# The end of two expert mixtures: residual rows reloaded before the last two scatters, whose rows TensorE places on their tokens with 0/1 matrices

## The chip, the cores and the metric

One core of one Trainium2 chip runs the whole program. The time is that of one execution in device microseconds; the kernel before has a median of 1824.23 us in 3 runs (1823.89 to 1829.28).

## The reference

Two layers of a transformer (a mixer and a mixture of experts each) are followed by a third block. There are 512 tokens of width 1024, all in float32. The mixture and what follows it:

```python
x = x + g_f * hierarchical_moe(hf, ...)          # 16 experts, two per token
# inside: hid = silu(t @ w_gate) * (t @ w_up);  y = (hid * gate) @ w_down
hm = rmsnorm(x, norm_mix[1]) * (1 + sc_m) + sh_m  # next layer: x feeds a norm at once
y = forgetting_mixer(hm, b_w_in, ...)             # projection by b_w_in
...
h = rmsnorm(x, norm_g)                            # after the second mixture: second_block
proj = h @ w_in + b_in
```

So each mixture ends in a sum over tokens (x plus the experts' rows), and what follows normalises that sum and multiplies it by a weight matrix. There are two such places in the program. The **first end** lies between the first mixture and `mix_b` (the second layer's mixer, about 905 to 960 us), the **second end** between the second mixture and `block2` (about 1455 to 1500 us).

## The kernel before, in words

Tokens stand in four tiles of 128 rows (x0 to x3, here also tile 0 to tile 3). `moe` runs 17 steps; step e computes the hidden layer of expert e and then, in `expert_out`, the output rows of expert e-1. An expert has at most 96 tokens (`CAP`); their numbers are the column `tidx` of that expert. The output rows `y` (96 x 1024) go out on POOL's queue by an indirect DMA that adds them in memory to the residual array `xd`:

```python
self.scatter(R["xd"], idx, y)      # last line of expert_out
```

The 16 scatters follow one another, since all of them add to `xd`. "Scatter 13" below is that of expert 13, and 14 and 15 are the last two.

After the mixture `normed_T` loads the four tiles from `xd` into new buffers `xl` (SP's queue), multiplies each by the norm's row (DVE, `hn`), takes the squares' sum on ACT (`tn_j`, in `tile_norm`), scales `hn` on DVE, and hands it to `transpose_tile`: eight transposes on PE (`tp`), then for each half the upper part of the split on ACT (`hThi`) and the lower part on DVE (`hTlo`). The next phase multiplies these by weights that are split alike: a staged tile `wst` (loaded on SP's queue) becomes `whi` on ACT (L316) and `wlo` on DVE (L317). In `mix_b` a unit is four such tiles of 128x768 and there are four `wst` buffers (`weight_pool(4, 8)`); in `block2` a tile is 128x1024 and there are three (`weight_pool(3, 5)`). w0 and w1 are the first two units. In `mix_b` w0 meets tile 0 alone and then both meet tile 1 and tile 2; in `block2` the first products need tiles 0 and 1 together (256 columns).

SP's queue issues the loads in program order, and each engine its own instructions in the order that the scheduler has fixed beforehand (PE's by hand). Memory of closed pools is used again: the first writer of a new tile waits for whatever still uses the old one.

Of the kernel before, what the change touches and what calls it, by code (L numbers as in the profile page):

```python
# [20 lines left out]
S = 512  # L21
# [91 lines left out]
class Kernel:  # L113
# [948 lines left out]
                res.append([hi, lo])  # L1062
        return res

    def expert_out(self, pool, hT, d, idx, gate, R):

        nc, q = self.nc, self.CAP
        y = self.t(pool, [q, D], F32, "y", 4)
        for n in range(2):
            p = self.sc()[:q]  # L1070
            ns = slice(n * 512, (n + 1) * 512)
            for j in range(2):
                h, w = hT[j], d[j][0]
# [148 lines left out]
    def moe(self, R, after):  # L1222
# [3 lines left out]
        with ExitStack() as ctx:  # L1226
# [27 lines left out]
                self.token_gates(ohs, [R["tg"][:, t, e, 2:5] for t in range(NT)], gates[:, e:e + 1], self.CAP)  # L1254

            xs = {}

            def step(e, ohs):
                if e < 16:
                    w = self.W[e]  # L1260
                    p = self.mm()
                    self.expert_part(p, xs[e], w, range(4))
                    if e < 15:
                        xs[e + 1] = self.expert_in(pm, xgs[(e + 1) % 3])
                    self.expert_part(p, xs.pop(e), w, range(4, KC))
                    listed(e + 3, True)
                    hid = self.expert_hidden(pm, p)
                if e:
                    w = self.W[e - 1]
                    self.expert_out(pm, self.hT, w[4:], idx[:, e - 1:e], gates[:, e - 1:e], R)  # L1270
                if e < 16:
                    self.hT = self.expert_hidden_T(pm, hid, self.W[e])
                    load(6)
# [14 lines left out]
            with self.tc.manual_schedule(engines={mybir.EngineType.PE}):  # L1288
                for e in range(17):
# [3 lines left out]
                    if e == 15:  # L1293
                        self.ln_table = None
                        self.need_ln(self.last_act)
        self.rt_ctx.close()
        return R["xd"]

    def normed_T(self, pool, xd, rows, hT):

        nc = self.nc
        xs = []
        for t in range(NT):
            xs.append(self.t(pool, [P, D], F32, "xl", NT))
            self.x_ins = nc.sync.dma_start(xs[t], xd[t * P:(t + 1) * P, :])
        yield
        for t, x in enumerate(xs):
            h = self.t(pool, [P, D], F32, "hn", 2)
            nc.vector.tensor_mul(h, x, rows[0])
            r = self.tile_norm(pool, x)  # L1310
            if rows[1] is None:
                nc.vector.tensor_scalar(h, h, r, None, op0=ALU.mult)
            else:
                nc.vector.scalar_tensor_tensor(h, h, r, rows[1], op0=ALU.mult, op1=ALU.add)
            self.transpose_tile(h, hT, t)
            yield

    def close_rows(self):
        self.rp_ctx.close()
        self.rp = None  # L1320

# [107 lines left out]
        yield from self.attn_values(pool, "b", blocks, hs, terms, lambda h, o: nc.scalar.activation(oT[hs[h], hp], o, AF.Copy))  # L1429
        u["done"] = 2  # L1430

    def mix_b(self, xd, rows):
        nc = self.nc
        w = self.a["b_w_in"]
        NC = 3 * D + 16
        unit = lambda hp: self.w_unit(w, hp * P, NC, D)
# [5 lines left out]
        with ExitStack() as ctx:  # L1442
# [13 lines left out]
            with self.tc.manual_schedule(engines={mybir.EngineType.PE}):  # L1456
                with ExitStack() as c2:
                    pn = self.pool(c2, "pn")
                    w0 = unit(0)
                    split(w0)  # L1460
                    tiles = self.normed_T(pn, xd, rows, hT)
# [377 lines left out]
                yield 1.25 * m  # L1839
        return p[:, :m]  # L1840

    def block2(self, xd, grow):
        nc, a = self.nc, self.a
        ud = self.t(self.dp, [4 * P, 4, P], F32, "ud")
        yd = self.t(self.dp, [4 * P, 4, P], F32, "yqd")
        bcol = lambda blk: self.vcol("bin")[:, blk:blk + 1]
        with ExitStack() as ctx:
# [16 lines left out]
            with self.tc.manual_schedule(engines={mybir.EngineType.PE}):  # L1864
# [4 lines left out]
                with ExitStack() as c2:  # L1869
# [1 line left out]
                    todo = []  # L1871
                    w0 = self.proj_w(0, todo)
                    split(todo)
                    tiles = self.normed_T(pn, xd, (grow, None), hT)
# [225 lines left out]
    def right_pools(self):  # L2100
# [5 lines left out]
        self.ws = self.pool(self.rt_ctx, "ws", "right")  # L2106

    def load_x(self, pool, src):
        xs = []
# [99 lines left out]
    def start(self, ctx):  # L2209
        self.pools(ctx)  # L2210
        self.rp_ctx = ctx.enter_context(ExitStack())
        self.rt_ctx = ctx.enter_context(ExitStack())
        self.rp, self.ln_table = None, None
        self.have_params = False
        self.wp_ctx = ctx.enter_context(ExitStack())
# [37 lines left out]
```

## Time and profile before

| | us |
|---|---|
| median of 3 runs | 1824.23 |
| lowest and highest | 1823.89, 1829.28 |
| the profiled execution | 1824.57 |
| its span | 1822.6 |
| PE busy | 1624.6 (89%) |
| DVE, ACT, POOL busy | 1285.6, 919.7, 123.9 |

The profiled execution is 0.34 us above the median, so its rows can stand for all of them. PE has most of the busy time, but the share is a mean: at both ends of a mixture PE stands still while the residual goes out, comes back and is normalised. Times in the trace count from the span's start.

### The profile page before, as it was taken

What the parts mean: (1) busy time and instruction counts of PE and PEld (TensorE: products, weight loads), DVE (VectorE), ACT (ScalarE), POOL (GpSimd) and SP (SyncE); (2) the same over time, 40 slices, a digit from 0 to 9 for tenths busy, and PEclk for the clock granted to TensorE, in tenths of its full rate; (3) what the DMA queues carried; (4) which work ended last, traced back from release to release, by engine and by line L of the source; (5) the groups of instructions that cost most, each with busy time, mean ns of one, the idle gap of its engine ahead of it and who ended that gap; (6) DMA issues with size and microseconds to landing.
All of it is one profiled execution on the core that took longest, in us unless ns stands there. A gap on an engine that the chain in (4) does not pass through costs nothing. (4 is left out here: it accounts for less than half of the span.)

```text
span 1822.6 us, 29089 instructions
## 1 busy us (share of the span) xinstructions
PE 1624.6 (89%) x10222; PEld 1381.7 (76%) x10223; DVE 1285.6 (71%) x3181; ACT 919.7 (50%) x1975; POOL 123.9 (7%) x101
## 2 busy tenths in 40 slices
PE   5979999999999998699859999898689959999998
PEld 3778999989989987456548798887455647788886
DVE  6758677677776656688755768757688746998564
ACT  4536455565555652566533655642556534353443
POOL 1000000000000000133210000000132210000000
PEclk9999999999999998799989999999799979999999
DMA  8786546466564235799872231226799854233331
GB/s 291 225 282 206 170 146 195 148 180 187 153 182 120 84 100 193 235 306 323 271 185 71 71 89 51 76 82 208 232 315 314 266 168 116 78 106 99 111 117 72
DMA packets 263995, 310.90 MB, mean 171 GB/s; under 512 B 33887, under 2 KB 177867, under 8 KB 263836
## 3 DMA queue, kind: packets, MB, share of 16 engines
q1 hardware_dynamic: 255708, 291.89, 51.1%
q0 software_dynamic: 8128, 17.02, 4.2%
q8 instruction: 84, 1.38, 0.3%
q14 instruction: 75, 0.61, 0.1%
HBM read 287.88 MB, written 38.90 MB: 179 GB/s over the span
## 5 line engine op out<-in xcount | busy, mean ns | idle before, releaser
L154 PE MATMUL mm<-whi,hThi 128*128 128x384 f32 (+2 forms) x1128 | 401.7, 356 | 5.4 <-DVE vlo L420 2.5
L154 PE MATMUL mm<-whi,hTlo 128*128 128x384 f32 (+2 forms) x1128 | 382.4, 339 | 0.8 <-DVE hTlo L741 0.6
L154 PE MATMUL mm<-wlo,hThi 128*128 128x384 f32 (+2 forms) x1128 | 381.1, 338 | 0.0
L317 DVE TENSOR_TENSOR wlo<-wst,whi 128x768 fp32r<-128x768 f32 (+2 forms) x200 | 199.6, 1009 | 69.4 <-ACT whi L316 66.9
L154 PEld LDWEIGHTS mm<-whi,hThi 128*128 128x128 f32 x1128 | 214.2, 190 | 15.0 <-DVE vlo L420 3.1
L316 ACT ACTIVATE whi<-wst 128x768 fp32r<-128x768 f32 (+2 forms) x200 | 176.1, 890 | 92.7 <-PE mm L154 54.3
L317 DVE TENSOR_TENSOR ehl<-est,ehl 128x1024 fp32r<-128x1024 f32 x144 | 175.7, 1220 | 61.5 <-ACT ehl L316 47.2
L154 PEld LDWEIGHTS mm<-whi,hTlo 128*128 128x128 f32 x1128 | 213.9, 190 | 4.4 <-DVE hTlo L741 1.8
L154 PEld LDWEIGHTS mm<-wlo,hThi 128*128 128x128 f32 x1128 | 214.8, 190 | 1.9 <-issue 0.6
L316 ACT ACTIVATE ehl<-est 128x1024 fp32r<-128x1024 f32 x144 | 152.1, 1058 | 110.5 <-DMA est<-in_w_up_dram 44.1
L249 DVE SCALAR_TENSOR_TENSOR adacc<-ast,csil,adacc 128x512 f32<-128x512 f32 x168 | 125.9, 750 | 66.0 <-DMA ast<-in_w_ada_dram 64.2
L154 PE MATMUL mm<-ehl,xTh 128*96 128x512 f32 x480 | 153.3, 400 | 0.0
L154 PE MATMUL mm<-hThi,whi 128*128 128x512 f32 (+1 forms) x288 | 107.1, 372 | 0.7 <-ACT sza L1925 0.6
L154 PE MATMUL mm<-hTlo,whi 128*128 128x512 f32 (+1 forms) x288 | 105.9, 368 | 0.5 <-DVE hTlo L311 0.3
L154 PE MATMUL mm<-hThi,wlo 128*128 128x512 f32 (+1 forms) x288 | 105.7, 367 | 0.0
L416 ACT ACTIVATE raw<-mm 128x256 f32<-128x256 f32 x126 | 47.9, 380 | 108.4 <-PE mm L154 108.0
L421 DVE TENSOR_REDUCE qss<-sq 128x4 f32<-128x256 f32 x128 | 52.9, 413 | 61.6 <-ACT sq L418 61.4
L154 PE MATMUL mm<-ehl,xTl 128*96 128x512 f32 x240 | 94.8, 395 | 0.0
L154 PEld LDWEIGHTS mm<-ehl,xTh 128*96 128x96 f32 x480 | 73.2, 162 | 25.8
L489 DVE TENSOR_TENSOR pTl<-tp,pTh 128x512 fp32r<-128x512 f32 (+1 forms) x112 | 68.4, 628 | 23.3 <-ACT pTh L488 22.6
L154 PE MATMUL av<-pTh,vhi 128*64 128x128 f32 x400 | 77.7, 230 | 0.4 <-ACT pTh L488 0.4
L487 PE MATMUL tp<-cst,pexp 128*128 128x128 f32 x400 | 64.2, 279 | 15.4 <-DVE pTl L489 11.7
(474 smaller groups left out, 3393.0 us busy)
## 6 DMA issues: line engine op xcount, KB each, us to landing
ast<-in_w_ada_dram SPq DMA_DIRECT2D x192, 256.0 KB
wst<-in_a_w_in_dram SPq DMA_DIRECT2D x192, 192.0 KB
est<-in_w_gate_dram SPq DMA_DIRECT2D x124, 256.0 KB
est<-in_w_up_dram SPq DMA_DIRECT2D x124, 256.0 KB
wst<-in_w_in_dram SPq DMA_DIRECT2D x32, 512.0 KB
est<-in_w_down_dram SPq DMA_DIRECT2D x30, 512.0 KB
esp<-in_w_down_dram SPq DMA_DIRECT2D x30, 512.0 KB
wst<-in_b_w_in_dram SPq DMA_DIRECT2D x64, 192.0 KB
```

Source lines behind the costliest of these rows:

```text
L154: self.nc.tensor.matmul(out, lhsT=l, rhs=r, start=n_first and i == 0, stop=n_last and i == nt - 1)
L249: last = nc.vector.scalar_tensor_tensor(acc, st, self.csil[:, k:k + 1], acc, op0=ALU.mult, op1=ALU.add)
L316: nc.scalar.activation(hi, st, AF.Copy)
L317: nc.vector.tensor_sub(lo, st, hi.bitcast(F32))
L416: nc.scalar.activation(raw[:, t].rearrange("p a b -> p (a b)"), p[:, :256], AF.Copy)
L421: nc.vector.tensor_reduce(ss[:, 4 * t:4 * t + 4], sq.rearrange("p (g d) -> p g d", d=HD), axis=AX.X, op=ALU.add)
L487: nc.tensor.transpose(p[:, j * q:(j + 1) * q], blocks[c + j], self.ident[:q, :q])
L489: self.mark = nc.vector.tensor_sub(lo[:, :m * q], p[:, :m * q], hi[:, :m * q].bitcast(F32))
```

## The change

`moe` now keeps the tiles of x in SBUF over its end. After the output of expert 13 (step 14), x0 to x3 are loaded from `xd` into buffers `x0` to `x3` that staged weights have left free. For experts 14 and 15 `expert_out` also splits `y` into an upper part (ACT) and a lower part (DVE); `expert_places` makes from `tidx` four 96x128 matrices of 0 and 1 for each of the two experts; `tail_sums` multiplies them on PE (32 products of 512 columns) into eight PSUM banks, two for each token tile. `normed_T` loads nothing: it adds the banks to the x tiles (eight additions of 128x512 on DVE) and goes on as before. Scatters 14 and 15 stay, since `xd` is read again later.

```diff
     def expert_out(self, pool, hT, d, idx, gate, R, parts=None):
...
             nc.vector.scalar_tensor_tensor(y[:, ns], p, gate, R["grow"][:q, ns], op0=ALU.mult, op1=ALU.mult)
+            if parts is not None:
+                nc.scalar.activation(parts[:q, 0, ns], y[:, ns], AF.Copy)
+                nc.vector.tensor_sub(parts[:q, 1, ns], y[:, ns], parts[:q, 0, ns].bitcast(F32))
         self.scatter(R["xd"], idx, y)
+
+    def expert_places(self, pool, tail, idx):
+
+        nc, q = self.nc, self.CAP
+        f = self.t(pool, [q, 1], F32, "tidf", 2)
+        nc.vector.tensor_copy(f, idx)
+        oh = self.t(self.wp, [P, 2, D], F32R, "ehl", self.NHL)[:q, 0, :S]
+        for t in range(NT):
+            nc.vector.tensor_scalar(oh[:, t * P:(t + 1) * P], self.iota[:q], 128.0 * t - 1.0, f, op0=ALU.add, op1=ALU.is_equal)
+        tail["oh"].append(oh)
+
+    def tail_sums(self, tail, i, ts):
+
+        q = self.CAP
+        for t in ts:
+            if i == 0:
+                tail["ps"][t] = [f() for f in ((self.tp, self.tp), (self.sc, self.sc), (self.sc, self.av), (self.mm, self.mm))[t]]
+            for h in range(2):
+                for j in range(2):
+                    self.nc.tensor.matmul(tail["ps"][t][h], lhsT=tail["oh"][i][:, t * P:(t + 1) * P],
+                                          rhs=tail["rows"][i][:q, j, h * 512:(h + 1) * 512],
+                                          start=i == 0 and j == 0, stop=i == 1 and j == 1)
...
+                if e == 14:
+                    for t in range(NT):
+                        x = self.t(self.px, [P, D], F32, f"x{t}")
+                        self.x_ins = nc.sync.dma_start(x, R["xd"][t * P:(t + 1) * P, :])
+                        tail["x"].append(x)
+                if e == 15:
+                    for i in (14, 15):
+                        self.expert_places(pm, tail, idx[:, i:i + 1])
...
-        self.rt_ctx.close()
-        return R["xd"]
+                self.tail_sums(tail, 0, (0, 3))
+                self.tail_sums(tail, 1, (0,))
+                self.tail_sums(tail, 0, (1, 2))
+                self.tail_sums(tail, 1, (1, 2, 3))
+        self.ws_ctx.close()
+        return R["xd"], tail
...
-            xs.append(self.t(pool, [P, D], F32, "xl", NT))
-            self.x_ins = nc.sync.dma_start(xs[t], xd[t * P:(t + 1) * P, :])
+        def add(t):
+            for i in range(2):
+                n = slice(i * 512, (i + 1) * 512)
+                nc.vector.tensor_add(tail["x"][t][:, n], tail["x"][t][:, n], tail["ps"][t][i])
...
+            if t == 0:
+                add(0)
             h = self.t(pool, [P, D], F32, "hn", 2)
...
             self.transpose_tile(h, hT, t)
+            if t == 0:
+                for i in range(1, NT):
+                    add(i)
             yield
 
     def close_rows(self):
+        self.rt_ctx.close()
```

The order of instructions moves at three places. On SP's queue at the first end the loads of x (`xl`) stood behind the four tiles of w0; lines are those of each kernel's own file. Before:

```order
L331 DMA wst_2388_11251<-in_b_w_in_dram 128x3x128 x2
L331 DMA wst_2391_11256<-in_b_w_in_dram 128x3x128 x2
L331 DMA wst_2394_11261<-in_b_w_in_dram 128x3x128 x2
L331 DMA wst_2397_11266<-in_b_w_in_dram 128x3x128 x2
L1305 DMA xl_2398_11277<-xd0_1649_8236 128x1024
L1305 DMA xl_2399_11279<-xd0_1649_8236 128x1024
L1305 DMA xl_2400_11281<-xd0_1649_8236 128x1024
L1305 DMA xl_2401_11283<-xd0_1649_8236 128x1024
L331 DMA wst_2404_11287<-in_b_w_in_dram 128x3x128 x2
L331 DMA wst_2407_11292<-in_b_w_in_dram 128x3x128 x2
```

With the change:

```order
L1303 DMA x0_2362_11134<-xd0_1649_8236 128x1024
L1303 DMA x1_2363_11136<-xd0_1649_8236 128x1024
L1303 DMA x2_2364_11138<-xd0_1649_8236 128x1024
L1303 DMA x3_2365_11140<-xd0_1649_8236 128x1024
L331 DMA wst_2406_11321<-in_b_w_in_dram 128x3x128 x2
L331 DMA wst_2409_11326<-in_b_w_in_dram 128x3x128 x2
L331 DMA wst_2412_11331<-in_b_w_in_dram 128x3x128 x2
L331 DMA wst_2415_11336<-in_b_w_in_dram 128x3x128 x2
L1378 DMA wf_2478_11662<-in_b_w_in_dram 128x8x16
L1381 DMA fb_2479_11664<-in_b_f_bias_dram 16x1
L331 DMA wst_2418_11349<-in_b_w_in_dram 128x3x128 x2
L331 DMA wst_2421_11354<-in_b_w_in_dram 128x3x128 x2
```

The loads of x now come first. The tiles of w0 (`wst_2406` to `wst_2415`) follow them, and those of w1 (from `wst_2418`) come after two small loads.

On ACT at the second end, with what each instruction waits for (DMASW names are POOL's DMAs, the scatters among them; DMAHW names SP's). Before:

```order
L316 ACTIVATE whi_3843_17975<-wst_3845_17977 128x1024 [waits DMASW1_49,DMASW2_49,DMASW0_49,DMASW3_49,SP_sequencer_49,DMASW4_49,DVE_sequencer_49,DMASW5_49,PE_sequencer_49,DMASW6_49,Activation_sequencer_49,DMASW7_49,Pool_sequencer_49,DMA
L293 ACTIVATE tn_j_3862_18006,tn_ss_3861_18005<-xl_3846_17983 128x1024 [waits DMAHW6_49,DMAHW2_49]
L293 ACTIVATE tn_j_3870_18035,tn_ss_3869_18034<-xl_3847_17985 128x1024 [waits DMAHW7_49,Activation_49]
L167 ACTIVATE tn_r_3864_18010<-tn_v_3863_18008 128x1 [waits DVE_49]
L168 ACTIVATE tn_r_3864_18010<-tn_r_3864_18010 128x1 [waits Activation_49]
L167 ACTIVATE tn_r_3872_18039<-tn_v_3871_18037 128x1 [waits DVE_49]
L293 ACTIVATE tn_j_3882_18172,tn_ss_3881_18171<-xl_3848_17987 128x1024 [waits DMAHW0_49]
L168 ACTIVATE tn_r_3872_18039<-tn_r_3872_18039 128x1 [waits Activation_49]
L167 ACTIVATE tn_r_3884_18176<-tn_v_3883_18174 128x1 [waits DVE_49]
L168 ACTIVATE tn_r_3884_18176<-tn_r_3884_18176 128x1 [waits Activation_49]
L293 ACTIVATE tn_j_3890_18201,tn_ss_3889_18200<-xl_3849_17989 128x1024 [waits DMAHW1_49]
L310 ACTIVATE hThi_3833_17953<-tp_3866_18018 128x4x128 [waits DMASW5_49,DMASW4_49,DMASW6_49,DMASW3_49,DMASW7_49,DMASW1_49,PE_49]
```

With the change:

```order
L168 ACTIVATE tn_r_3892_18146<-tn_r_3892_18146 128x1 [waits Activation_49]
L293 ACTIVATE tn_j_3898_18177,tn_ss_3897_18176<-x1_3827_17930 128x1024 [waits DMAHW5_49,DVE_49]
L293 ACTIVATE tn_j_3910_18314,tn_ss_3909_18313<-x2_3828_17932 128x1024 [waits DMAHW6_49,DVE_49,Activation_49]
L310 ACTIVATE hThi_3865_18095<-tp_3894_18154 128x4x128 [waits DMASW4_49,DMASW3_49,DMASW5_49,DMASW2_49,DMASW6_49,DMASW1_49,DMASW7_49,DMASW0_49,PE_49]
L310 ACTIVATE hThi_3865_18095<-tp_3895_18161 128x4x128 [waits PE_49]
L293 ACTIVATE tn_j_3918_18343,tn_ss_3917_18342<-x3_3829_17934 128x1024 [waits DMAHW7_49,DVE_49,Activation_49]
L316 ACTIVATE whi_3872_18113<-wst_3874_18115 128x1024 [waits DMAHW0_49]
L316 ACTIVATE whi_3875_18117<-wst_3877_18119 128x1024 [waits DVE_sequencer_49,SP_sequencer_49,PE_sequencer_49,DMAHW1_49,Activation_sequencer_49,Pool_sequencer_49]
L316 ACTIVATE whi_3878_18125<-wst_3880_18127 128x1024 [waits DMAHW2_49]
L167 ACTIVATE tn_r_3900_18181<-tn_v_3899_18179 128x1 [waits DVE_49]
```

Splits of w0 (`whi`, L316) stood ahead of the first `tn_j` (the first row of before is one) and stand behind both halves of `hThi` now. The first `hThi` waits for POOL's DMAs, scatters 14 and 15 among them; before, both were in by then, since the `xl` loads behind them had landed.

On DVE at the second end, from the scaling of tile 0 on before:

```order
L1312 TENSOR_SCALAR hn_3860_18003<-hn_3860_18003,tn_r_3864_18010 128x1024
L295 TENSOR_SCALAR tn_v_3883_18174<-tn_ss_3881_18171 128x1
L169 TENSOR_TENSOR tn_t_3873_18040<-tn_r_3872_18039 128x1
L170 SCALAR_TENSOR_TENSOR tn_t_3873_18040<-tn_t_3873_18040,tn_v_3871_18037 128x1
L171 SCALAR_TENSOR_TENSOR tn_r_3872_18039<-tn_t_3873_18040,tn_r_3872_18039 128x1
L169 TENSOR_TENSOR tn_t_3885_18177<-tn_r_3884_18176 128x1
L1312 TENSOR_SCALAR hn_3868_18032<-hn_3868_18032,tn_r_3872_18039 128x1024
L170 SCALAR_TENSOR_TENSOR tn_t_3885_18177<-tn_t_3885_18177,tn_v_3883_18174 128x1
L171 SCALAR_TENSOR_TENSOR tn_r_3884_18176<-tn_t_3885_18177,tn_r_3884_18176 128x1
L295 TENSOR_SCALAR tn_v_3891_18203<-tn_ss_3889_18200 128x1
L1309 TENSOR_TENSOR hn_3880_18169<-xl_3848_17987,rs_3663_17242 128x1024
L311 TENSOR_TENSOR hTlo_3834_17954<-tp_3866_18018,hThi_3833_17953 128x4x128
```

With the change, from tile 1's multiplication (behind tile 0's two `hTlo`) on:

```order
L1354 TENSOR_TENSOR hn_3896_18174<-x1_3827_17930,rs_3677_17314 128x1024
L317 TENSOR_TENSOR wlo_3873_18114<-wst_3874_18115,whi_3872_18113 128x1024
L317 TENSOR_TENSOR wlo_3876_18118<-wst_3877_18119,whi_3875_18117 128x1024
L295 TENSOR_SCALAR tn_v_3899_18179<-tn_ss_3897_18176 128x1
L1354 TENSOR_TENSOR hn_3908_18311<-x2_3828_17932,rs_3677_17314 128x1024
L169 TENSOR_TENSOR tn_t_3901_18182<-tn_r_3900_18181 128x1
L317 TENSOR_TENSOR wlo_3879_18126<-wst_3880_18127,whi_3878_18125 128x1024
L170 SCALAR_TENSOR_TENSOR tn_t_3901_18182<-tn_t_3901_18182,tn_v_3899_18179 128x1
L295 TENSOR_SCALAR tn_v_3911_18316<-tn_ss_3909_18313 128x1
L295 TENSOR_SCALAR tn_v_3919_18345<-tn_ss_3917_18342 128x1
L171 SCALAR_TENSOR_TENSOR tn_r_3900_18181<-tn_t_3901_18182,tn_r_3900_18181 128x1
L1357 TENSOR_SCALAR hn_3896_18174<-hn_3896_18174,tn_r_3900_18181 128x1024
```

Tile 1 was scaled (the second L1312 row) ahead of tile 0's `hTlo`; now its scaling (L1357, the last row) comes behind tile 0's `hTlo` and three `wlo`.

## Rows read from the trace of the kernel before

**Rows 1.** Windows after the ends: us, each engine's busy us (instructions), clock, DMA share, GB/s.

```profile
960.00:1100.00 140.00, 132.05 (x993) 117.64 (x992) 95.14 (x294) 75.48 (x197) 0.00 (x0) 0.99 0.28 77
...
1600.00:1822.00 222.00, 213.82 (x1024) 178.34 (x1022) 152.37 (x335) 92.99 (x140) 0.00 (x0) 0.99 0.32 101
```

**Rows 2.** Timeline, PE: start us, us, line, operation, out and in, idle before and releaser.

```profile
944.19 1.11 PE L308 MATMUL tp<-cst,hn 128*128 128x128 f32 x4 [18.35 <-DVE hn L1314]
...
951.46 1.03 PE L308 MATMUL tp<-cst,hn 128*128 128x128 f32 x8
...
1486.15 1.97 PE L308 MATMUL tp<-cst,hn 128*128 128x128 f32 x8 [16.30 <-DVE hn L1312]
```

**Rows 3.** Chain that ended last, second end: start us, us, what.

```profile
1457.25 5.55 PE mm L154 x24
...
1466.98 5.26 DMA xd<-y,tidx
...
1472.99 5.30 DMA xd<-y,tidx
1478.31 0.34 SPq L1305
...
1492.63 7.43 PE mm L154 x54
```

**Rows 4.** Timeline, POOL: the scatters of both ends.

```profile
914.14 1.40 POOL L971 DMA_INDIRECT xd<-y,tidx  x1 [7.09 <-DVE hTl L1061]
922.97 1.40 POOL L971 DMA_INDIRECT xd<-y,tidx  x1 [7.43 <-DVE hTl L1061]
...
929.22 1.55 POOL L971 DMA_INDIRECT xd<-y,tidx  x1 [3.47 <-DMA xd<-y,tidx]
...
1458.15 1.40 POOL L971 DMA_INDIRECT xd<-y,tidx  x1 [7.09 <-DVE hTl L1061]
```

**Rows 5.** All 32 scatters of experts' rows by line: ns least/median/most, first and last start.

```profile
L971 POOL DMA_INDIRECT xd<-y,tidx x32: 1403/2076/2805, 769.2 to 1473.0; - x32
```

**Rows 6.** Timeline, SP's queue: weight and x loads of both ends.

```profile
925.01 4.47 SPq L331 DMA_DIRECT2D wst<-in_b_w_in_dram  x6
...
935.95 1.76 SPq L1305 DMA_DIRECT2D xl<-xd  x4
937.81 7.72 SPq L331 DMA_DIRECT2D wst<-in_b_w_in_dram  x8
...
1465.09 0.93 SPq L340 DMA_DIRECT2D wst<-in_w_in_dram  x2
```

**Rows 7.** Timeline, ACT: first end, then the first upper half of the second.

```profile
931.86 0.84 ACT L316 ACTIVATE whi<-wst 128x768 fp32r<-128x768 f32 x1 [7.99 <-DMA wst<-in_b_w_in_dram]
...
944.53 1.06 ACT L293 ACTIVATE tn_j<-xl 128x1024 f32<-128x1024 f32 x1 [0.22 <-DMA xl<-xd]
...
945.68 0.57 ACT L310 ACTIVATE hThi<-tp 128x512 fp32r<-128x512 f32 x1
...
1487.80 0.58 ACT L310 ACTIVATE hThi<-tp 128x512 fp32r<-128x512 f32 x1
```

**Rows 8.** Timeline, DVE: first end, then second.

```profile
948.63 3.55 DVE L317 TENSOR_TENSOR wlo<-wst,whi 128x768 fp32r<-128x768 f32 x4
...
1465.95 0.75 DVE L1076 SCALAR_TENSOR_TENSOR y<-sc,gates,rg 96x512 f32<-96x512 f32 x1 [0.81 <-PE sc L154]
1466.62 0.24 DVE L1061 TENSOR_TENSOR hTl<-tp,hTh 128x96 fp32r<-128x96 f32 x1
...
1470.55 2.35 DVE L317 TENSOR_TENSOR wlo<-wst,whi 128x1024 fp32r<-128x1024 f32 x2
1481.96 1.23 DVE L1309 TENSOR_TENSOR hn<-xl,rs 128x1024 f32<-128x1024 f32 x1 [9.06 <-issue]
...
1489.30 1.28 DVE L311 TENSOR_TENSOR hTlo<-tp,hThi 128x512 fp32r<-128x512 f32 x2
```

**Rows 9.** The token lists' 0/1 matrices by line: ns least/median/most.

```profile
L948 DVE TENSOR_TENSOR oh<-cst,rt_rk x32: 542/548/552, 731.7 to 1404.5; 128x384 bf16<-128x384 f32 x32
```

More of the change, by code (lines that the diff above doesn't have):

```diff
@@ L1063, in expert_hidden_T, with expert_out @@
         return res
-    def expert_out(self, pool, hT, d, idx, gate, R):
+    def expert_out(self, pool, hT, d, idx, gate, R, parts=None):
         nc, q = self.nc, self.CAP
@@ L1256, in moe @@
             xs = {}
+            tail = dict(oh=[], rows=[], ps={}, x=[])
             def step(e, ohs):
@@ L1269, in step @@
                     w = self.W[e - 1]
-                    self.expert_out(pm, self.hT, w[4:], idx[:, e - 1:e], gates[:, e - 1:e], R)
+                    parts = self.t(self.wp, [P, 2, D], F32R, "ehl", self.NHL) if e > 14 else None
+                    self.expert_out(pm, self.hT, w[4:], idx[:, e - 1:e], gates[:, e - 1:e], R, parts)
+                    if e > 14:
+                        tail["rows"].append(parts)
+                if e == 14:
[6 more added lines that the diff above has]
+                        self.expert_places(pm, tail, idx[:, i:i + 1])
                 if e < 16:
@@ L1295, in moe, with normed_T @@
                         self.need_ln(self.last_act)
-        self.rt_ctx.close()
-        return R["xd"]
-    def normed_T(self, pool, xd, rows, hT):
+                self.tail_sums(tail, 0, (0, 3))
[4 more added lines that the diff above has]
+        return R["xd"], tail
+    def normed_T(self, pool, tail, rows, hT):
         nc = self.nc
-        xs = []
-        for t in range(NT):
-            xs.append(self.t(pool, [P, D], F32, "xl", NT))
-            self.x_ins = nc.sync.dma_start(xs[t], xd[t * P:(t + 1) * P, :])
+        def add(t):
+            for i in range(2):
+                n = slice(i * 512, (i + 1) * 512)
+                nc.vector.tensor_add(tail["x"][t][:, n], tail["x"][t][:, n], tail["ps"][t][i])
         yield
-        for t, x in enumerate(xs):
+        for t, x in enumerate(tail["x"]):
+            if t == 0:
+                add(0)
             h = self.t(pool, [P, D], F32, "hn", 2)
@@ L1430, in forget_values, with mix_b @@
         u["done"] = 2
-    def mix_b(self, xd, rows):
+    def mix_b(self, x, rows):
         nc = self.nc
+        xd, tail = x
         w = self.a["b_w_in"]
@@ L1460, in mix_b @@
                     split(w0)
-                    tiles = self.normed_T(pn, xd, rows, hT)
+                    tiles = self.normed_T(pn, tail, rows, hT)
                     next(tiles)
@@ L1840, in colmm, with block2 @@
         return p[:, :m]
-    def block2(self, xd, grow):
+    def block2(self, x, grow):
         nc, a = self.nc, self.a
+        xd, tail = x
         ud = self.t(self.dp, [4 * P, 4, P], F32, "ud")
@@ L1873, in block2 @@
                     split(todo)
-                    tiles = self.normed_T(pn, xd, (grow, None), hT)
+                    tiles = self.normed_T(pn, tail, (grow, None), hT)
                     next(tiles)
@@ L2105, in right_pools @@
         self.px = self.pool(self.rt_ctx, "px", "right")
-        self.ws = self.pool(self.rt_ctx, "ws", "right")
+        self.ws = self.pool(self.ws_ctx, "ws", "right")
     def load_x(self, pool, src):
@@ L2212, in start @@
         self.rt_ctx = ctx.enter_context(ExitStack())
+        self.ws_ctx = ctx.enter_context(ExitStack())
         self.rp, self.ln_table = None, None
```

## The prediction

> **What bounds the kernel now.** I read the windows first. Away from the ends of the mixtures PE is busy 132 of 140 us and 214 of 222 us [rows 1], so what an end loses or gains is carried to the last instruction nearly whole. Then PE's timeline at the two ends: PE stands still 18.35 us at the first and 16.30 us at the second, in both until DVE has normalised tile 0 [rows 2]. The chain of the second end says what fills that wait: scatter 14 (5.26 us), scatter 15 (5.30 us), the load of x, the norm, and the first dense products at 1492.63 [rows 3]. The reader should see one queue of things that can't overlap: both scatters and the reload add to or read the same `xd`. Weights are no part of the wait before: w0 is loaded and split while the scatters run (loads from 925.01 and 1465.09 [rows 6], splits from 931.86 and 1470.55 [rows 7, 8]).
>
> **The second end, step by step.**
>
> *x early.* The reload may start when scatter 13 is in. It starts on POOL at 1458.15 [rows 4]; with 5.3 us like its followers [rows 3] it is in at 1463.45. In the kernel before, the first tile can be read 3.65 us after the first issue (1478.31 [rows 3] to 1481.96 [rows 8]) and the last one 8.6 us after it (935.95 [rows 6] to 944.53 [rows 7]). So x3 is there at about 1472.05. It is hidden behind experts 14 and 15.
>
> *The scatters move back.* Scatter 14 adds to the memory that these four loads read, so it can't start at 1466.98 any more but at 1472.05. With the durations and the gap of the chain (5.26, 0.75, 5.30 [rows 3]) scatter 15 is in at 1483.4, 5.1 us later than before. The order listing of ACT shows who waits for that: the first `hThi` takes memory that the `y` rows held, and waits for both. So the scatters are taken from x's path and put on that of the transposed tile.
>
> *PE's part.* On DVE eight 0/1 matrices and two lower parts of `y` now stand ahead of the last `hTl`. A 128x384 matrix of 0 and 1 costs 0.548 us [rows 9]; for 96x128 I take 0.2, between a 96-column `hTl` at 0.24 [rows 8] and a third of 0.548 (0.18); the bounds 0.15 and 0.55 move the sum by less than 3 us. Lower parts cost half a `wlo`, 0.6 [rows 8]. 8 x 0.2 + 2 x 0.6 = 2.8, less the 0.81 that DVE idles between the two `y` [rows 8]: PE ends the last expert 2.0 us later, near 1471.8. The last `y`, its two parts (0.75 + 0.6 + 0.6) and the first of the 32 placing products (0.23 each by 24 in 5.55 us [rows 3]) give x0's sum at about 1474.6. Two additions at 0.64 (priced as `hTlo`, which also reads PSUM [rows 8]): 1476.0. From there tile 0 needs 4.2 us to the transposes as before (1481.96 [rows 8] to 1486.15 [rows 2]) plus some 0.5 us for additions that slip in: 1480.7, done near 1482.6. `hThi` waits for scatter 15: 1483.4, against 1487.80 before [rows 7]. **Tile 0 gains 4.4 us.**
>
> *The queue behind it.* The first products need tile 1 too, and here the order turns. Splits of w0 stood ahead of `tn_j`; now three stand behind `hThi`, on a queue that only moves when scatter 15 lands, and DVE has them ahead of tile 1's scaling. By the rows in the order listing, each at its own price: `hThi` 0.5, two `hTlo` 1.28, `hn` of tile 1 1.2, two `wlo` 2.35, `hn` of tile 2 1.2, one `wlo` 1.17, small ones 0.5, scaling 0.8 [rows 7, 8]: 9.0 us, so 1483.4 + 9.0 = 1492.4 for tile 1's transposes. Two more `wlo` (2.35) stand ahead of its `hTlo`: 1492.4 + 2.35 + 0.3 = 1495.0, and the first products follow 0.7 later at 1495.7, against 1492.63 before [rows 3]. **The second end loses 3.1 us.** What comes late next is the weights: with three staging buffers the fourth tile is loaded only after the first `wlo`.
>
> **The first end.** By the same steps: scatter 13 at 914.14 [rows 4] is in at 919.4, x3 at 928.0 (8.6 us). Scatter 14 took 6.25 us to the next one's start [rows 4], scatter 15 took 6.7 us to the issue behind it (929.22 [rows 4] to 935.95 [rows 6]): 941.0. With 5.3 us and the second end's gap it would be 939.4. I take 940.2. `hThi` of tile 0 is then 5.5 us earlier than its 945.68 [rows 7]. But w0's tiles are now loaded behind the placing products (near 932 instead of 925.01) and split behind `hThi`; and w1's four tiles, which were issued from 937.81 [rows 6] on, each need a staging buffer that a `wlo` of w0 frees. The first is freed at 940.2 + 0.5 + 1.28 + 1.2 + 0.9 = about 943.5 (its own split 0.84 beside it), the third one at about 946. Three `wlo` of w1 stand ahead of tile 1's scaling. The third's load takes between 3.65 us (the first x tile, above) and 6.85 us (925.01 [rows 6] to 931.86 [rows 7]): landed 949.7 to 952.9, `whi` 0.84, `wlo` 0.89 [rows 8], scaling 1.3: tile 1's transposes at 952.7 to 955.9, against 951.46 [rows 2]. That is 1.2 to 4.4 us later; I take 3.3, above the middle, since scatter 15's tail shares the DMA engines with these loads. **The first end loses 3.3 us.**
>
> **At no cost.** Placing products on PE (32 x 0.23 = 7.4 us an end) lie in PE's idle time; ACT's copies of `y` and DVE's additions lie in the 9 us that DVE idled [rows 8]. Without the wait for the scatters the additions would show, 5.1 us an end. The memory for x is there already. On POOL small loads of masks move behind scatter 15; nothing early reads them.
>
> **Sum.** 1824.57 + 3.1 + 3.3 = **1831.0 us**; the profiled execution is 0.34 us above the median, which I leave in.
>
> **Rivals.**
>
> *Tile 1 isn't held (faster).* If the staged weights were split before `hThi` after all, or the loads of w1 were quick, the gain of tile 0 would be carried: 4.4 and 5.5 us, 1824.6 - 9.9 = 1814.7. It decides from the point where tile 1's scaling follows tile 0's `hTlo` within 4 us. Against it: the order on ACT and DVE is fixed, and both count 9 us of work at the second end. For it: the additions leave tiles 1 to 3 ready, so later tiles wait less. Chance 0.15.
>
> *Gain and loss cancel.* Scatters at the short price (939.4), loads at 3.65 us and products that catch up on tiles 2 and 3, which are ready: between 1 us gained and 1 us lost at each end, 1823 to 1827, say 1826. For it: DMA is idle at that time but for w0. Chance 0.23.
>
> *Scatters slow down on POOL.* The four scatters here that met an idle DVE took 1.40 to 1.55 us on POOL [rows 4]; over all 32 the median is 2.08 and the most 2.81 [rows 5]. Both scatters now meet a DVE that works, so up to 1.4 us each can be added before `hThi`, 2.8 an end: 1831.0 + 5.6 = 1836.6. Against it: most of DVE's work there reads PSUM. Chance 0.15. The Trainium skill ("SBUF — State Buffer", section "Who interferes with whom") has DVE and GpSimd share one pair of SBUF ports under an exclusive lock, so that descriptors of a POOL transfer wait for some DVE operations; it speaks against this change, and [rows 5] agrees that scatters differ by a factor of two, though not with which operation.
>
> *Scatters at a shorter price.* The chain's 5.26 and 5.30 us [rows 3] decide above. A scatter cheaper by 2.4 us would free `hThi` before its transposes are done, and each end would lose 1.7 us less (1483.4 to 1481.7): 1827.6. Nothing in the rows speaks for it; chance 0.05. The Trainium skill ("DMA: Bandwidth & Descriptors", section "Anatomy of one DMA — SWDGE (gpsimd) path") gives about 2.0 us plus bytes over 436 GB/s for a transfer from that queue, an estimate of 2.9 us for 96 rows of 4 KB, and by it the time would be that 1827.6; the chain's rows of this kernel, whose scatters add in memory, don't agree.
>
> **How the numbers follow.** The forecast as worked out has 0.42; its own range is 1827.5 to 1834 by the bounds of the first end's load and scatters. Some 0.3% (5.5 us) is what a measurement of this kernel can tell from no change, so between 1818.7 and 1829.7 counts as same. Of the forecast about a quarter lies below 1829.7; with the cancelling case and the shorter scatters that is 0.23 + 0.10 + 0.05 = 0.38, less 0.02 for their edge: same 0.36. Slower: 0.32 + 0.15 + 0.02 = 0.49. Faster: 0.15. The range leaves about 0.1 below (most of the faster case) and 0.1 above (the worst of slow scatters): 1816.5 to 1837.0.
>
> **What would show it.** Right: loads of x issued near 919 and 1463; scatter 15 in near 940 and 1483; `hThi` of tile 0 waiting for DMA `xd` with its transposes done; DVE with `wlo` between tile 0's `hTlo` and tile 1's scaling; first products of the second end near 1495, tile 1's transposes of the first near 955, with what the first end lost added to the second's times. Wrong: `hThi` that follows its transposes at once, tile 1's transposes under 4 us behind tile 0's, or PE's idle time at the two ends together below 30 us.

## The result, and the profile after

The changed kernel took **1839.01 us** (median of 5 runs, 1836.53 to 1840.70) against 1824.23 us for the kernel before (now the median of 5 runs, 1822.05 to 1832.52): ratio **1.0067**, interval 1.0046 to 1.0087, so 8 to 16 us slower. The forecast, 1831.0 us, had the sign and about half the size; the measured median lies above its own range (1827.5 to 1834) and above the top of the wider one (1837.0); the ratio, put on the 1824.57 us that the forecast starts from, gives 1836.8.

All landmarks below are counted from one anchor in each mixture's end, the last expert's first output product, because what came earlier differs by some microseconds from run to run: at scatter 13 of the first end, ahead of anything that the change touches, the changed kernel was already 2.28 us later (916.42 against 914.14 [rows 4]). Timeline of PE in the kernel before: the anchor and the third tile's transposes, first and second end.

```profile
922.42 0.71 PE L154 MATMUL sc<-ehl,hTh 128*96 128x512 f32 x2 [0.34 <-ACT hTh L1060]
961.88 1.04 PE L308 MATMUL tp<-cst,hn 128*128 128x128 f32 x8
...
1466.42 0.71 PE L154 MATMUL sc<-ehl,hTh 128*96 128x512 f32 x2 [0.34 <-ACT hTh L1060]
1504.82 1.03 PE L308 MATMUL tp<-cst,hn 128*128 128x128 f32 x8
```

The same of the changed kernel, with the transposes of tiles 0 and 1 and the first dense products that need tile 1 (1506.92), which answer to [rows 2] and to the last of [rows 3].

```profile
924.70 0.71 PE L154 MATMUL sc<-ehl,hTh 128*96 128x512 f32 x2 [0.34 <-ACT hTh L1060]
939.50 1.09 PE L308 MATMUL tp<-cst,hn 128*128 128x128 f32 x8 [1.71 <-DVE hn L1359]
945.92 0.69 PE L154 MATMUL mm<-whi,hThi 128*128 128x384 f32 x1 [5.34 <-ACT whi L316]
958.71 1.32 PE L308 MATMUL tp<-cst,hn 128*128 128x128 f32 x8 [4.42 <-DVE hn L1359]
971.60 1.03 PE L308 MATMUL tp<-cst,hn 128*128 128x128 f32 x8
...
1474.03 0.71 PE L154 MATMUL sc<-ehl,hTh 128*96 128x512 f32 x2 [0.34 <-ACT hTh L1060]
1488.33 1.09 PE L308 MATMUL tp<-cst,hn 128*128 128x128 f32 x8 [1.18 <-DVE hn L1357]
1503.04 1.94 PE L308 MATMUL tp<-cst,hn 128*128 128x128 f32 x8 [13.62 <-DVE hn L1357]
1506.92 0.58 PE L154 MATMUL mm<-hTlo,whi 128*128 128x256 f32 x1 [0.80 <-DVE hTlo L311]
1520.79 1.03 PE L308 MATMUL tp<-cst,hn 128*128 128x128 f32 x8
```

Counted from the anchor, tile 0's transposes start 7.0 us sooner than before at the first end (14.80 against 21.77) and 5.4 us sooner at the second (14.30 against 19.73), and are over long before anything uses them: at the second end PE then stands for 13.62 us until DVE has scaled tile 1. By tile 2 the first end has lost 7.44 us (46.90 against 39.46) and the second 8.36 us (46.76 against 38.40). With the 2.28 us from upstream, less some 2.1 us that the second mixture, which waits for its weights, took up again, this is 16.0 of the 16.2 us between the two profiled spans (1838.8 and 1822.6).

What holds tile 1 stands in the chain that ended last, second end of the changed kernel (start us, us, what).

```profile
1485.69 0.45 issue
1486.14 7.73 DMA xd<-y,tidx
...
1494.47 0.59 ACT hThi L310
1495.06 1.03 ACT tn_j L293 x2
1496.10 0.95 ACT whi L316
...
1498.22 1.22 DVE wlo L317
...
1499.47 4.46 DMA wst<-in_w_in_dram
1503.95 1.07 ACT whi L316
1505.04 1.23 DVE wlo L317
1506.26 0.61 DVE hTlo L311
```

Scatter 15 takes 7.73 us where it took 5.30 [rows 3]; `hThi` waits for it; behind `hThi` come splits, a late weight tile, another split, and only then tile 1's `hTlo`. POOL's timeline of the changed kernel has scatters 14 and 15 at both ends, and ACT's the first `hThi` with its wait:

```profile
931.32 1.40 POOL L971 DMA_INDIRECT xd<-y,tidx  x1 [13.50 <-DVE y L1076]
937.30 1.40 POOL L971 DMA_INDIRECT xd<-y,tidx  x1 [4.57 <-DVE tn_t L170]
...
1480.32 1.40 POOL L971 DMA_INDIRECT xd<-y,tidx  x1 [13.16 <-DVE ehl L1079]
1486.14 1.40 POOL L971 DMA_INDIRECT xd<-y,tidx  x1 [4.42 <-DVE tn_t L169]
...
944.54 0.60 ACT L310 ACTIVATE hThi<-tp 128x512 fp32r<-128x512 f32 x1 [5.07 <-DMA idh<-in_c_tab_dram]
...
1493.98 1.08 ACT L310 ACTIVATE hThi<-tp 128x512 fp32r<-128x512 f32 x2 [5.13 <-DMA xd<-y,tidx]
```

DVE's timeline of the second end's stretch shows the queue: nothing runs for 5.14 us, and then one instruction behind the other, tile 1's scaling (1502.14) last.

```profile
1488.19 1.28 DVE L1347 TENSOR_TENSOR x<-x,mm 128x512 f32<-128x512 f32 x2
1494.61 1.29 DVE L311 TENSOR_TENSOR hTlo<-tp,hThi 128x512 fp32r<-128x512 f32 x2 [5.14 <-ACT hThi L310]
1495.82 1.22 DVE L1354 TENSOR_TENSOR hn<-x,rs 128x1024 f32<-128x1024 f32 x1
1497.08 2.36 DVE L317 TENSOR_TENSOR wlo<-wst,whi 128x1024 fp32r<-128x1024 f32 x2
...
1500.62 1.22 DVE L317 TENSOR_TENSOR wlo<-wst,whi 128x1024 fp32r<-128x1024 f32 x1
...
1502.14 0.75 DVE L1357 TENSOR_SCALAR hn<-hn,tn_r 128x1024 f32<-128x1024 f32 x1
```

### The profile page after: what moved, and what is told of

It is laid out like the page before. It is cut to its first block, busy times and chain, and to the rows that moved or that the text cites. A ratio compares the mean times of both kernels' runs of the same rounds, so it can differ in the third digit from the quotient of the medians.

```text
span 1838.8 us, 29264 instructions
## 1 busy us (share of the span) xinstructions
PE 1647.1 (90%) x10286; PEld 1400.6 (76%) x10287; DVE 1302.2 (71%) x3225; ACT 924.2 (50%) x1983; POOL 126.6 (7%) x101
## 5 line engine op out<-in xcount | busy, mean ns | idle before, releaser
L316 ACT ACTIVATE whi<-wst 128x768 fp32r<-128x768 f32 (+2 forms) x200 | 175.8, 891 | 87.4 <-PE mm L154 54.7
L316 ACT ACTIVATE ehl<-est 128x1024 fp32r<-128x1024 f32 x144 | 152.2, 1058 | 108.7 <-DMA est<-in_w_up_dram 42.9
L154 PE MATMUL av<-pTl,vhi 128*64 128x128 f32 x400 | 78.0, 230 | 3.0 <-DVE pTl L489 3.0
```

The lines of the kernel that those rows point to most:

```text
L154: self.nc.tensor.matmul(out, lhsT=l, rhs=r, start=n_first and i == 0, stop=n_last and i == nt - 1)
L316: nc.scalar.activation(hi, st, AF.Copy)
```

## The experiments

Theory after the result: two things make the loss together, the wait of `hThi` for scatters 14 and 15, and the order of DVE (VectorE) and ACT (ScalarE) behind it, in which splits of dense weights stand between tiles 0 and 1. Rivals: one of the two alone, or the added work alone. The table has every kernel: us from the anchor to the third tile's transposes at the first and second end, what both ends lose against before, and the measured ratio with its interval.

| kernel | first | second | lost | ratio |
|---|---|---|---|---|
| before | 39.46 | 38.40 | | 1 |
| changed | 46.90 | 46.76 | 15.8 | 1.0067 (1.0046 to 1.0087) |
| e1_no_scatter | 43.09 | 41.17 | 6.4 | 1.0024 (1.0002 to 1.0045) |
| e2_weights_free | 44.08 | 43.85 | 10.1 | 1.0058 (1.0036 to 1.0079) |
| e3_no_placing | 41.82 | 38.98 | 2.9 | 1.0024 (1.0005 to 1.0043) |
| e4_store | 45.31 | 44.67 | 12.1 | 1.0046 (1.0026 to 1.0066) |
| e6_priority | 40.08 | 41.06 | 3.3 | 1.0019 (1.0002 to 1.0037) |
| e7_no_wait_priority | 44.41 | 41.68 | 8.2 | 1.0027 (1.0007 to 1.0047) |
| b0_f32 | 40.97 | 36.79 | -0.1 | 0.9999 (0.9982 to 1.0016) |
| b1_f32_priority | 43.62 | 39.75 | 5.5 | 1.0017 (0.9996 to 1.0038) |
| p0_before_priority | 42.22 | 41.81 | 6.2 | 1.0021 (1.0005 to 1.0038) |
| b3_f32_late_tiles | 49.70 | 39.51 | 11.4 | 1.0059 (1.0040 to 1.0078) |

What the two ends lose by tile 2 orders the kernels nearly as the ratios do, so most of the loss is made there. Each row's ends come from one traced execution, for b1 and b3 the longest of the kernel's 12 and 8 (1838.07 and 1842.5 us), so rows that lie within a few us of one another can't be ranked.

**e1_no_scatter**: the last two scatters left out.

```diff
-        self.scatter(R["xd"], idx, y)
+        if parts is None:
+            self.scatter(R["xd"], idx, y)
```

> The changed kernel without scatters 14 and 15 at both ends (their rows are missing in xd, which later phases read; all else is there, and the order on ACT and DVE is the changed kernel's: w0 is split behind hThi). Theory A (hThi waits for scatter 15, and a queue of splits starts behind it): hThi starts right behind tile 0's transposes, about 3.9 us earlier than in the changed kernel at the first end and 4.6 us at the second, and about 8 us come back: ratio to before 1.001 to 1.003. Rival B (only the late loads and splits of w0 and w1 hold tile 1): hThi is earlier, but tile 1's transposes stay within 2 us of where they were, ratio 1.005 to 1.007. Rival C (the added work on DVE, ACT and PE): no difference to the changed kernel.

`hThi` came 17.04 and 14.96 us after the anchor, straight behind its transposes, where the changed kernel had 19.84 and 19.95: the wait is 2.8 and 5.0 us. The queue behind it stayed as long (14.2 and 9.06 us to tile 1's transposes, in both kernels). Without the wait 9.4 of the 15.8 us are gone; 6.4 stay.

**e2_weights_free**: the placing matrices and parts get memory of their own, so that w0's loads are issued early again.

```diff
-        oh = self.t(self.wp, [P, 2, D], F32R, "ehl", self.NHL)[:q, 0, :S]
+        if not tail["oh"]:
+            tail["place"] = self.t(self.ws, [P, 1, D], F32R, "est", DL["nes"])
...
-                    parts = self.t(self.wp, [P, 2, D], F32R, "ehl", self.NHL) if e > 14 else None
+                    parts = [self.t(self.ws, [P, 1, D], F32R, "est", DL["nes"])[:, 0] for _ in range(2)] if e > 14 else None
```

> The changed kernel with the 0/1 matrices and the parts of y in the buffers of staged expert weights, so that the first load of w0 doesn't wait for the placing products; scatters and the wait of hThi stay. Theory A: w0 is loaded some 10 us earlier and split ahead of hThi, tile 1 is scaled before hThi starts; hThi still waits for scatter 15 at both ends (by at least 2 us); tile 1's transposes follow it within 4 us instead of 14 and 9: about 6 to 13 us come back, ratio 1.000 to 1.004. If the scatters' wait were all of it: ratio stays at 1.006 or above.

A miss: 1.0058 where 1.000 to 1.004 was expected. Weights came early (issued at 916.71, before the anchor), and little was gained: seven `wlo` between 934.64 and 944.3 now stand ahead of tile 1's scaling, five of them ahead of tile 0's, whose transposes come 24.85 us after the anchor in place of 14.80. ACT doesn't stand still before `hThi` here, since tile 0's transposes come later than scatter 15. So late weights alone are not the cause, and a loss of 10.1 us needs no wait: what stands ahead of the tiles on DVE is enough for it.

**e3_no_placing**: scatters and the early x stay; 0/1 matrices, parts, placing products and additions are left out.

```diff
-                if e == 15:
-                    for i in (14, 15):
-                        self.expert_places(pm, tail, idx[:, i:i + 1])
...
-                self.tail_sums(tail, 0, (0, 3))
```

> The changed kernel without the placing: no 0/1 matrices, no split of y, no products, no additions (the normalised x lacks the rows of experts 14 and 15); x is still loaded early and scatters 14 and 15 stay behind it. Theory A: hThi still waits for scatter 15, whose start is set by the load of x3, so most of the loss stays: ratio 1.001 to 1.006. Rival C (the added work on DVE, ACT and PE makes the loss): the loss is gone, ratio 0.998 or below.

The wait stayed (`hThi` idle for 9.6 us, 20.2 and 18.2 us after the anchor) and yet only 2.9 us are lost: with less work on DVE, the queue behind it is shorter (9.9 us at the first end). So the wait alone is not the loss either.

**e4_store**: memory as in e2, the last two scatters left out, and x's finished tiles stored to `xd`.

```diff
+            nc.gpsimd.dma_start(tail["xd"][t * P:(t + 1) * P, :], tail["x"][t])
```

> As e2, and in place of scatters 14 and 15 each tile of x is stored to xd after its additions by a plain transfer from POOL's queue, so nothing is left out. Theory A: both waits are gone; tile 0's transposes come some 6 us earlier than before the change at either end, hThi follows them at once with the weights split, so it is faster than before by 6 to 12 us: ratio 0.9935 to 0.997. Rival (the stores of 2 MB share the DMA engines with the loads of w1): 0.998 to 1.001.

A miss: 1.0046 where less than 1 was expected. Nothing waits for scatters here, but five splits of w0 and w1 at the first end and three at the second stand ahead of tile 0's scaling, as in e2. From here the order was the suspect.

**e6_priority**: the changed kernel whole, only the order of DVE and ACT is another (each tile's additions stand with its own steps, and these ahead of the splits).

```diff
         for t, x in enumerate(tail["x"]):
-            if t == 0:
-                add(0)
...
+            with self.tc.high_priority():
+                add(t)
```

> The changed kernel whole, with the scatters and the wait for them, but the steps of a tile (its two additions, its norm, its scaling, its transposes) are given a higher priority than the splits of the dense weights, so that on VectorE tile 1's scaling stands behind one hTlo of tile 0 and not behind two hTlo, an hn and two to four wlo. Nothing is left out. Theory (two terms, a wait for the scatters of 2.8 to 5 us an end and VectorE's order behind it): hThi comes as late as in the changed kernel, 19 to 20 us after the last expert's first output product, but tile 1's transposes follow it by 3 to 6 us instead of 14.2 and 9.06; ratio 1.001 to 1.005. Rival 1 (the order costs nothing, since w0 is bound anyway by its splits, and the dense products start when the last wlo of w0 is there): 1.006 to 1.009, as the changed kernel. Rival 2 (everything is in the order): 0.997 to 1.0.

This is the run that decides on the order. Windows from the anchor to tile 1 (first end: its transposes; second: the dense products that need it), then scatter 15's own stretch to `hThi` at the two ends: us, the busy us (instructions) of PE, PEld (PE's weight loads), DVE, ACT and POOL, clock, DMA share, GB/s. The first pair, of the kernel before:

```profile
922.42:951.46 29.04, 10.54 (x42) 7.92 (x43) 16.95 (x29) 13.39 (x28) 5.61 (x6) 0.71 0.79 201
...
1466.42:1492.63 26.21, 7.75 (x27) 4.88 (x28) 14.04 (x28) 11.90 (x26) 3.93 (x5) 0.64 0.63 195
```

Both pairs of the changed kernel:

```profile
924.70:958.71 34.01, 19.39 (x75) 14.62 (x75) 24.77 (x45) 15.51 (x30) 5.35 (x6) 0.85 0.75 190
1474.03:1506.92 32.89, 14.88 (x60) 10.11 (x60) 24.11 (x50) 14.87 (x29) 2.81 (x2) 0.77 0.57 174
...
937.30:944.54 7.24, 1.58 (x11) 0.92 (x9) 3.33 (x6) 1.95 (x4) 3.94 (x5) 0.85 1.05 228
1486.14:1493.98 7.84, 2.10 (x13) 1.36 (x11) 3.33 (x8) 2.30 (x5) 1.40 (x1) 0.86 0.73 214
```

Both with the tile steps first:

```profile
923.38:952.28 28.90, 19.82 (x74) 14.83 (x75) 24.53 (x50) 13.76 (x29) 5.36 (x6) 0.82 0.72 173
1463.23:1489.87 26.64, 15.36 (x58) 10.39 (x59) 22.67 (x48) 14.43 (x29) 2.81 (x2) 0.78 0.60 180
...
936.34:943.68 7.34, 2.10 (x9) 1.57 (x8) 6.74 (x19) 5.44 (x15) 3.95 (x5) 0.67 1.07 219
1475.38:1483.22 7.84, 2.91 (x13) 2.00 (x11) 7.14 (x18) 6.02 (x14) 1.40 (x1) 0.68 0.75 217
```

Scatter 15 and the wait are as long in both (7.24 and 7.84; 7.34 and 7.84). But DVE (third pair) is busy 3.33 us of the wait in the one and 6.74 and 7.14 us in the other. DVE's work up to tile 1 hardly differs (24.77 and 24.53; 24.11 and 22.67); where the work stands inside the wait, the stretch is 5.1 and 6.3 us shorter, and 12.5 of the 15.8 us are gone. At the first end w1's loads, which need the staging buffers that these splits free, are issued 18.8 us after the anchor in place of 23.2. Tile 1's transposes came 8.60 and 3.27 us behind `hThi`, where 3 to 6 was expected. Of the 3.3 us that stay, 3.0 lie behind tile 1: 0.76 at the first end, where PE waits 1.07 us for a `hTlo`, and 2.23 at the second, where the granted clock is 0.81 in place of 0.93.

**e7_no_wait_priority**: that order, no last scatters, and x stored as in e4 (diffs as above).

> As the run before, and without the scatters of experts 14 and 15: x's tiles, after their additions, are stored to xd as they are (four DMAs of 512 KB on GpSimd's queue, behind which nothing of the end waits), so that nothing waits for scatters and xd holds what the scatters would have left. Theory of two terms: both are gone; tile 1's transposes come 30 to 32 us (first end) and 23 to 26 us (second end) after the last expert's first output product, and the ratio is 0.998 to 1.002. Rival 1 (the order costs nothing): as the kernel with the same stores and the order left to itself in its own memory, 1.003 to 1.006. Rival 2 (the added work of VectorE and TensorE, some 10 us an end, is the bound however it is ordered): 1.002 to 1.004.

A miss: 1.0027, no better than the order alone, and inside the second rival's range. What e1 and e6 give back doesn't add up when both are done. At e7's first end a split on ACT waits 2.29 us for a tile of w0 with `hThi` behind it (PE waits 2.91 us), and another waits 1.29 us ahead of `hThi`'s second half. Four stores of 512 KB are issued beside those loads; that they make the loads late fits, but is not shown.

**b0_f32** and **b1_f32_priority**: placing products straight from `y` in float32, 0/1 matrices built two experts earlier, x stored; b1 with the tile steps first.

```diff
-                for j in range(2):
-                    self.nc.tensor.matmul(tail["ps"][t][h], lhsT=tail["oh"][i][:, t * P:(t + 1) * P],
...
+                self.nc.tensor.matmul(tail["ps"][t][h], lhsT=tail["oh"][i][:, t * P:(t + 1) * P],
+                                      rhs=tail["rows"][i][:, h * 512:(h + 1) * 512], start=i == 0, stop=i == 1)
```

> A leaner form of the change: no hi and lo parts of the rows (the placing products take y in float32, half as many of them but each slower), the 0/1 matrices built two experts earlier from the token numbers in float32, the products of tile 0 ahead of those of the other tiles, and the stores of x in place of the scatters of experts 14 and 15. The order of VectorE is left to itself. The dense weights' parts find their buffers free as in the kernel before, since the change takes none of them. Theory of two terms: no wait for scatters, and 4 to 6 us less work on VectorE and ScalarE ahead of tile 0, so 0.995 to 1.0. Rival 1 (the slow float32 products hold TensorE, 16 of some 0.9 to 1.8 us an end, and take the gain back): 1.0 to 1.005. Rival 2 (VectorE's order alone): as the next one is above it.

> The kernel of the run before with the steps of a tile ahead of the weight splits, as in the first run here. Theory of two terms: 0.993 to 0.999, at least 2 us below the run before. Rival 1 (float32 products hold TensorE): within 1 us of it, 1.0 to 1.005. Rival 2 (the dense products need w0's splits as much as tile 1, and now wait for those): tile 1's transposes are early, 22 to 26 us after the last expert's first output product, and the dense products start behind a wlo, 0.998 to 1.003.

b0 is the best form: 0.9999, all of the loss back, nothing gained beyond. Its second end is 1.6 us shorter than before and its first 1.5 us longer, since w0's first split comes behind the tile steps on ACT (PE waits 5.18 us for it). The priority that helps the changed kernel costs b1 some 3 us by the ratios and 5.6 by the ends, for the same reason (PE waits 4.12 us for that split, then 1.42 for its `wlo`); its interval touches no change, so this stands on the trace of its longest execution alone.

**p0_before_priority**: the kernel before with that priority (diff as in e6).

> The kernel before, with the tile steps given the higher priority over the weight splits as in the run of the changed kernel with that order; nothing else differs and nothing is left out. If the order is a loss that the change itself brings (the tile steps grew, so the splits fell between tile 0 and tile 1), the kernel before has little to gain from it: 0.999 to 1.001. Rival: the order is a lever of its own that had been lying unused, and then the changed kernel with priority must be held against this one: 0.995 to 0.998.

1.0021: slower, which neither had. That order is no lever of its own: PE's wait for tile 0 at the second end is 18.40 us in place of 16.30 [rows 2], and there is no added work to put into the wait for the scatters.

**b3_f32_late_tiles**: b0 with tiles 2 and 3 placed behind tile 0's transposes, and priority for w0's splits.

```diff
+                self.tail_sums(tail, 0, (2, 3))
+                self.tail_sums(tail, 1, (2, 3))
...
-                    split(w0)
+                    with self.tc.high_priority():
+                        split(w0)
```

> The leaner form (float32 placing products from y, the 0/1 matrices built early, x stored in place of the last two scatters), with the placing products of tiles 2 and 3 moved behind tile 0's transposes on TensorE, and the splits of w0 given priority. In the form without the move tile 0's transposes wait for all 32 placing products although tile 0's scaling is done 2.7 us (first end) and 4.5 us (second end) before. Theory (a queue of VectorE and ScalarE sets the end, and what goes ahead of tile 0 on TensorE delays it): tile 0's transposes 14 to 15 us and 13 to 14 us after the last expert's first output product in place of 17.0 and 17.0, the third tile's transposes 1 to 4 us earlier than in the form without the move, ratio 0.996 to 1.000. Rival (w0's splits and the dense products decide, and the placing products of tiles 2 and 3 now stand beside them): 0.999 to 1.003.

A miss that shows the mechanism by itself. Tile 0's transposes came as early as expected (14.0 and 11.8 us), and the kernel lost 11 us. ACT's timeline, first end:

```profile
937.51 1.06 ACT L293 ACTIVATE tn_j<-x 128x1024 f32<-128x1024 f32 x1 [1.70 <-DVE x L1342]
...
948.76 1.06 ACT L293 ACTIVATE tn_j<-x 128x1024 f32<-128x1024 f32 x1 [8.42 <-DVE x L1342]
...
949.82 1.06 ACT L310 ACTIVATE hThi<-tp 128x512 fp32r<-128x512 f32 x2
```

Tile 2's `tn_j` stands ahead of tile 0's `hThi` on ACT and waits 8.42 us for sums that PE now makes late; tile 0's transposes, done near 941, wait with it. Here the products were moved, and the queue was not: with the priority w0's first split still comes behind `hThi` at both ends (953.52 and 1505.55).

## Why the prediction was right, and where it fell short

Predicted times against measured ones, the measured moved back by what scatter 13 was late (2.28 us at the first end, 7.60 at the second):

| step | predicted | measured |
|---|---|---|
| x loads issued | 919.4, 1463.45 | 919.9, 1464.3 |
| scatter 14 starts | 928.0, 1472.05 | 929.0, 1472.7 |
| tile 0's transposes, second end | 1480.7 | 1480.7 |
| `hThi` of tile 0 | 940.2, 1483.4 | 942.3, 1486.4 |
| tile 1's transposes | 952.7 to 955.9, 1492.4 | 956.4, 1495.4 |
| first products, second end | 1495.7 | 1499.3 |

The steps of this table that missed all came later than predicted: no errors cancelled to give the sign, and it is the size that fell short.

- **The mechanism held.** x is hidden behind experts 14 and 15; `hThi` waits for scatter 15 through reused memory with its transposes done (idle 5.13 us at the second end, released by `xd`; at the first the profile names `idh`, a load issued behind scatter 15 on the same queue, and the two were not told apart). DVE's queue from `hThi` to tile 1's transposes was 9.06 us at the second end, 9.0 predicted, and 14.2 at the first, 12.5 to 15.7 predicted. (In the latter the first freed buffer, 940.2 + 0.5 + 1.28 + 1.2 + 0.9, comes to 944.1 and not 943.5; with that the range for tile 1's transposes is 953.3 to 956.5.) The small prices held too: 0.21 us a 0/1 matrix (0.2), 0.69 a lower part (0.6), 0.69 an addition (0.64), the last expert 1.9 us later (2.0).
- **Scatter 15 was mis-sized.** The step "with the durations and the gap of the chain (5.26, 0.75, 5.30)" took scatter 15's price from a stretch in which DMA had little else to do: in the kernel before, 36 GB/s moved during the second end's last scatter. The change itself lets w0's loads start in that stretch, and the price became 7.24 and 7.84 us at 228 and 214 GB/s. In e3, at 59 and 35 GB/s, it was 5.57 and 5.33, and in e2, whose w0 is loaded earlier, 5.17 at 36 GB/s at the second end. The changed kernel's 32 scatters say the same, from issue to landing: 5.1 and 5.2 us at 45 and 62 GB/s (scatter 14), 5.5 to 6.2 at 113 to 137, 6.9 and 7.7 at 230 and 217 (scatter 15), and 8.2 to 10.1 at 283 to 334 beside the experts' weights. So the chain's price was that of a quiet stretch. Its excess is 2.4 of the 3.6 us that the second end's products came later than predicted; 0.5 came with x's later loads and 0.6 with a weight tile behind tile 1's scaling. The prediction had named these loads, but as something that scatters delay.
- **The sum stopped at tile 1.** That is the larger miss: "the second end loses 3.1 us" and "the first end loses 3.3 us" take tiles 2 and 3 to follow as before. They didn't, though PE waited no more than 0.48 us there. Windows from tile 1's to tile 2's transposes (second end: from the first products), before:

```profile
951.46:961.88 10.42, 9.74 (x58) 9.15 (x57) 7.44 (x17) 2.64 (x8) 0.00 (x0) 1.00 0.49 135
1492.63:1504.82 12.19, 12.19 (x95) 12.19 (x96) 6.21 (x11) 3.32 (x6) 1.68 (x3) 0.93 0.49 141
```

  and after:

```profile
958.71:971.60 12.89, 12.41 (x56) 11.76 (x57) 7.36 (x17) 2.33 (x9) 0.00 (x0) 0.74 0.23 62
1506.92:1520.79 13.87, 13.87 (x95) 13.87 (x96) 3.44 (x6) 2.28 (x4) 0.24 (x2) 0.80 0.22 68
```

  The same products take 2.47 and 1.68 us longer, at a granted clock of 0.74 and 0.80 in place of 1.00 and 0.93: they come right after PE stood still for 4.42 and 13.62 us, where tile 1 had followed at once or after 2.01 us. At the first end they start 0.32 us apart until about 966.2 and some 0.17 us apart after it, at the lower of the clock's two levels (1.2 GHz) and then at the upper (2.4 GHz). 4.97 + 2.47 = 7.44 us at the first end, 6.68 + 1.68 = 8.36 us at the second. The ends lost 9.4 us more than forecast (15.8 against 6.4): 4.1 here, 3.6 up to the second end's first products, 1.7 up to the first end's tile 1.
- **The order was read rightly.** "Tile 1 isn't held" was put at 0.15 because the order on both engines is fixed; e6 shows that this order was worth 12.5 us, where e1, without the wait, gives back 9.4.
- **Rivals.** Gain and loss that cancel: not borne out, since it took the short scatter and products that catch up on tiles 2 and 3. Scatters that slow down on POOL: not borne out, scatters 14 and 15 took 1.40 us on POOL at both ends while DVE was busy for 5 of 6 us beside scatter 14. The exclusive port of the Trainium skill ("SBUF — State Buffer", "Who interferes with whom") is not seen in these four; a scatter 14 of e3 took 2.34 us on POOL, with a scaling of DVE beside it (second end, 1470.87), so for another order it isn't ruled out. Scatter 15 got longer behind POOL, on its way to memory. Shorter scatters: the estimate of 2.9 us from the Trainium skill ("DMA: Bandwidth & Descriptors", "Anatomy of one DMA — SWDGE (gpsimd) path") is below all 32 scatters of the changed kernel (5.1 to 10.1 us from issue to landing).
- **At no cost.** Placing products on PE were free, as said. DVE's additions were not quite: they lie in idle time, but up to tile 1 DVE is busy 24.77 and 24.11 us in place of 16.95 and 14.04, and e3, without that work, loses 2.9 us.

Left open: that w0's loads lengthen scatter 15 is read from stretches with different traffic. The first end of the kernel before fits (6.7 us to the load behind it, at 197 GB/s). Two scatters 14 of the second end don't: 5.26 us at 220 GB/s in the kernel before, with two tiles of w0 issued 1.9 us ahead of it, and 5.3 at 228 in e2. So the mean rate alone doesn't give the time. A changed kernel whose loads are held back until the scatter is in was not tried. No version beat the kernel before by more than a measurement can tell.

## What to carry to other kernels

When a change moves a wait from one instruction to another, list what is queued behind the new waiter on its engine, and put work that needs nothing from it ahead: here the ends lost 15.8 us or 3.3 us by the order alone, with the same scatter of 7 to 8 us in front. Price a transfer beside the traffic that the change lets start next to it, not in the quiet stretch where it ran before. And carry a loss on until the engine that sets the end runs as before, with its clock.

## What the runs showed of the hardware

The last scatter of 96 rows, which adds to memory, took 5.17 to 5.57 us with 35 to 59 GB/s on the core's DMA engines, 6.7 at 197 GB/s at the first end of the kernel before, and 7.24 to 7.84 at 214 to 228 GB/s beside weight loads of 192 and 512 KB; its time on POOL was 1.40 to 1.55 us in all of these. Over the changed kernel's 32 scatters the time to landing went from 5.1 us at 45 GB/s to 10.1 us at 331. Two scatters of 5.26 and 5.3 us at 220 and 228 GB/s, in other kernels, lie outside that order. PE's granted clock after an idle time of 4.42 us averaged 0.74 over the next 12.89 us, though PE was busy for 12.41 of them.
